# Four re-timings in an encoder trunk: a gate chunk ahead of the attention, decay tiles a score tile sooner, a seven-step age at the MLP's end, and one up chunk in token halves

## The chip, the cores and the metric

The kernel runs on one core of one Trainium2 chip. The time is the device time of that core from start to end of one execution, in microseconds (us); lower is better. The kernel before takes 1790.33 us, the median of three executions (1790.21 to 1791.44). Every duration below comes from one further execution, profiled, which took 1789.19 us with a span of 1787.3 us.

Engine names: PE multiplies matrices and transposes (a transposition is a matmul with the identity), DVE and ACT work elementwise (ACT with functions such as exp), POOL is a third elementwise engine, SP issues most of the DMA transfers. A PE matmul writes into a bank, a 128x512 buffer that ACT and DVE read; while nobody has read it, the bank can't be written again.

## The reference

Two layers over a residual stream h of 512 tokens by 1024 features. One layer computes:

```
u = RMSNorm(h)
q_a,k_a,v_a, q_r,k_r,v_r,g_r, gate_a,gate_b = split(u @ w_in)
A = dilated attention, 8 heads of 64; q,k rotated on 16 of 64 dims;
    three (window, dilation) groups merged by their softmax denominators
B = retention, 8 heads, both directions, each with its decay exp(log_gamma*(n-m));
    per-head GroupNorm, times silu(g_r)
m = sigmoid(gate_a) * (A @ w_att_out) + sigmoid(gate_b) * (B @ w_ret_out)
h = h + RMSNorm(m @ w_out)
h = h + RMSNorm(relu(RMSNorm(h) @ w_up)^2 @ w_down)        # 1024 -> 4096 -> 1024
h = h + sigmoid(RMSNorm(h) @ w_ple_gate) * RMSNorm(p[i] @ w_ple_proj)
```

All of it is float32 in and out.

## The kernel before

**Tiles and products.** The tokens lie in four tiles of 128. Each float32 operand is split into a high and a low part, and each product of a 128-deep slice takes three matmuls (high by high, high by low, low by high). Weights come as chunks of 128x1024: SP loads one (`raw`), ACT rounds it to its high part (L275), DVE or POOL forms the low part (L298). A normalised, transposed activation is `uT`: `pre_norm` (L372) normalises a token tile (`un`, L404, on DVE), and later PE transposes it in two quarters of four 128x128 blocks into the banks tp_83 and tp_84 (L412); ACT takes the high part out (L415) and DVE the low part (L416).

**Order.** PE executes its instructions in the order in which the program writes them. On the other engines a scheduler sets the order at build time from the dependences, its own estimates and priorities; at run time each engine then keeps that order. So moving something on PE can reorder DVE, ACT, POOL and SP.

**Steps.** A matmul job calls `step()` (L323) after every six matmuls. A step does two things. It takes the oldest queued transposes of a token tile if these were queued at least `age` steps ago (AGE in the input part, AGE_DN at the end of the MLP), and it lets a side generator go on by 0.94 units (`tick`). The side generator first runs the eight attention heads, then the eight retention heads; the pieces between its `yield`s stand on PE between the groups of six.

**The input part of a layer.** Value projection; four rope groups of the attention (each one two jobs of 24 matmuls, `t_job`, then rotations on DVE, L494 to L497, and a copy through DRAM by DMA). Then the side generator starts, and beside it run the main jobs: gate chunks `g_job` (24 matmuls each), four rope groups of the retention, its value projection, the output gates. One attention head (L538 on) is: four score tiles (L543, L544, two matmuls each, one step apart), for each the mask and row maximum on DVE (L547), exp with its sum on ACT (L548), reciprocal (L549) and scaling (L550) on DVE; then, a step later, four times four transposes of the scaled tiles (L562), one set of four in each step. Each set takes one block from all four scaled tiles. In every head but the first, the product with the values of the head before it (`pv`) takes the step between. One retention head: four score tiles times a decay tile (L612), the finish of the head before it (transposes at L594, L596, and the split of `retT`, L301), a product with the values, a copy of it to `yt` on ACT (L633), a step later its transposes (L638). The decay tile `T` of the next head (L581 to L587) takes POOL, DVE and at last exp on ACT (L586, 128x896).

**The MLP.** Four early up chunks (0 to 3), 28 more interleaved with seven-product matrix multiplications, then the last quarter of the down projection, `dn`, in plain form: the first half of the features for all tiles, the second half tile by tile, 24 matmuls each. After a tile's second half DVE takes the bank (L950), ACT squares (L348), DVE scales (L952) and adds to the residual (L943), ACT squares again, POOL forms 1/rms (L358), DVE normalises (L404). Its transposes follow AGE_DN steps after the tile was queued. Then comes the gate of the last block, `pg` (L319 on `uT`), tiles 0 and 1 first, in alternation, in layer 0. DN_GRP, EARLY and the ages are constants at L41 to L52. The products between (`product`, L866) also step with AGE_DN, with nothing queued at that time. EARLY is the number of first up chunks whose matmuls are done in two halves of 256 tokens (L888, 24 per half and chunk) and not in full width (24 of 512, L309).

Of the kernel before, what the change touches and what calls it, by code (L numbers as in the profile page):

```python
# [42 lines left out]
DN_GRP = ONES  # L43
PG_GRP = (PAIRS, ONES, PAIRS, ((0, 1), (2,)))
AGE = 7
AGE_DN = 6
AGE_PG = (8, 7)
AGE_VA = 7
START = (3, 5, 7)
AGE_PP = 8  # L50
EARLY = 3
EARLY_BANKS = ("s", "acc", "acc")  # L52
ROPE_POOL = ()
POOL_LOW = ("qa", "ka", "qr", "kr", "vr", "g", "ga", "ao")
# [142 lines left out]
def block(ctx: ExitStack, tc: tile.TileContext, x, pT, w, dl, gains, cs, lc, rel, eye, out):  # L197
# [306 lines left out]
    def load_qk(i, mix, h):  # L504
        g, hh = divmod(h, 4)
        q, k = stage[i, mix, g, "q"], stage[i, mix, g, "k"]
        qs = tmp.tile([P, S], F32R, name="qs", tag="qs", bufs=2)
        kk = blk("R", [P, 2, S], F32R, name="kk")
        for o in range(2):
            for hl in range(2):  # L510
                p0 = hl * 64 + o * 32
                nc.sync.dma_start(qs[p0:p0 + 32, :].bitcast(F32), q[o, hh * 32:(hh + 1) * 32, hl, :])
                nc.sync.dma_start(kk[p0:p0 + 32, :, :].bitcast(F32), k[o, hh * 32:(hh + 1) * 32, :, :])
        return qs, kk

    def att_heads(i, va, lct, attT):
        part = [None]
        qk = load_qk(i, 0, 0)

        def pv(h, pt):  # L520
            o = bank("tp")
            for k in range(NT):
                v = va[k][:, h, :, :].rearrange("p a d -> p (a d)")
                for hl in range(2):
                    nc.tensor.matmul(o, lhsT=v, rhs=pt[k][:, hl, :], start=k == 0 and hl == 0, stop=k == 3 and hl == 1)  # L525
            if h % 2 == 0:
                part[0] = t2("part")
            c = t2("cross")
            me, other = slice(64 * (h % 2), 64 * (h % 2) + 64), slice(64 - 64 * (h % 2), 128 - 64 * (h % 2))
            nc.scalar.activation(c[me], o[other], AF.Copy)  # L530
            nc.vector.tensor_tensor(part[0][me], o[me], c[me], op=ALU.add)
            if h % 2:
                b = blk("A", [P, 2, S], F32R, name="attT")
                split(b, part[0])
                attT.append(b)

        late = None
        for h in range(8):  # L538
            qs, kk = qk
            zs = []  # L540
            for t in range(NT):
                ps = bank("s")
                nc.tensor.matmul(ps, lhsT=qs[:, t * P:(t + 1) * P], rhs=kk[:, 0, :], start=True, stop=False)  # L543
                nc.tensor.matmul(ps, lhsT=qs[:, t * P:(t + 1) * P], rhs=kk[:, 1, :], start=False, stop=True)  # L544
                z = t2("z")
                nm, den, rd = col(name="nm"), col(name="den"), col(name="rd")
                nc.vector.tensor_tensor_reduce(z, ps, lct[t // 2][:, t % 2, :], -0.125, 3.0e38, ALU.add, ALU.min, nm)  # L547
                nc.scalar.activation(z, z, AF.Exp, bias=nm, scale=-1.0, accum_out=den)  # L548
                nc.vector.reciprocal(rd, den)  # L549
                nc.vector.tensor_scalar(z, z, rd, 0.5, op0=ALU.mult, op1=ALU.mult)  # L550
                zs.append(z)
                if t == 0 and h < 7:
                    qk = load_qk(i, 0, h + 1)
                yield 1
            if late:
                pv(*late)
            yield 1
            pt = []
            for k in range(NT):
                ps = bank("tp")  # L560
                for t in range(NT):
                    nc.tensor.transpose(ps[:, t * P:(t + 1) * P], zs[t][:, k * P:(k + 1) * P], ident)  # L562
                b = blk("P", [P, 2, S], F32R, name="pt")
                split(b, ps)
                pt.append(b)
                yield 1
            late = (h, pt)
        yield 1
        pv(*late)
        yield 1  # L570

    def load_v(i, h):
        v = blk("V", [P, NT, 2 * P], F32R, name="vh")
        nc.sync.dma_start(v.bitcast(F32), stage[i, "v", h // 4][:, :, h % 4, :].rearrange("t p e -> p t e"))
        return v

    def ret_heads(i, relt, gT, retT):
        late = None
        qk, vh = load_qk(i, 1, 0), load_v(i, 0)

        def decay(h):  # L581
            T = blk("X", [P, 896], name="T")
            T2 = blk("P", [P, 896], name="T2")
            nc.gpsimd.tensor_scalar(T2, relt, nlg[:, i * 16 + 8 + h:i * 16 + 9 + h], 1.0, op0=ALU.mult, op1=ALU.mult)
            nc.vector.scalar_tensor_tensor(T, relt, lg[:, i * 16 + h:i * 16 + h + 1], T2, op0=ALU.mult, op1=ALU.min)
            nc.scalar.activation(T, T, AF.Exp)  # L586
            return T  # L587

        Tn = decay(0)

        def finish(h, y3):
            ps = bank("tp")
            for t in range(NT):
                nc.tensor.transpose(ps[:, t * P:(t + 1) * P], y3[:, t, :], ident)  # L594
            z = t2("yz")
            nc.vector.tensor_tensor(z, ps, gT[h], op=ALU.mult)  # L596
            b = blk("A", [P, 2, S], F32R, name="retT")
            split(b, z, sub=nc.gpsimd if FIN_POOL else None)
            retT.append(b)

        for h in range(8):
            qs, kk = qk
            v = vh
            T = Tn
            rt = []
            for k in range(NT):
                ps = bank("s")
                nc.tensor.matmul(ps, lhsT=kk[:, 0, k * P:(k + 1) * P], rhs=qs, start=True, stop=False)  # L608
                nc.tensor.matmul(ps, lhsT=kk[:, 1, k * P:(k + 1) * P], rhs=qs, start=False, stop=True)  # L609
                z = t2("rz")  # L610
                o = 384 - P * k
                nc.vector.tensor_tensor(z, ps, T[:, o:o + S], op=ALU.mult)  # L612
                b = blk("P", [P, 2, S], F32R, name="rt")
                split(b, z, sub=nc.gpsimd if k in RT_POOL else None)
                rt.append(b)
                if k == 0 and h < 7:
                    qk, vh = load_qk(i, 1, h + 1), load_v(i, h + 1)
                yield 1
            if late:
                finish(*late)  # L620
            yield 1
            if h < 7:
                Tn = decay(h + 1)
            y = t2("y")
            y3 = y.rearrange("p (t e) -> p t e", t=NT)
            o = bank("tp")
            n = 0
            for k in range(NT):
                for a, b in HL:
                    nc.tensor.matmul(o, lhsT=v[:, k, a * P:(a + 1) * P], rhs=rt[k][:, b, :], start=n == 0, stop=n == 11)  # L630
                    n += 1
            yt = t2("yt")
            nc.scalar.activation(yt, o, AF.Copy)  # L633
            yield 1
            o = bank("tp")
            o3 = o.rearrange("p (t e) -> p t e", t=NT)
            for t in range(NT):
                nc.tensor.transpose(o3[:, t, :], yt[:, t * P:(t + 1) * P], ident)  # L638
            mv = sm.tile([P, NT, 2], F32, name="mv", tag="mv", bufs=3)
            for t in range(NT):  # L640
                st = sm.tile([P, 6], F32, name="st", tag="st", bufs=4)
                nc.vector.bn_stats(st, o3[:, t, :])
                nc.vector.bn_aggr(mv[:, t, :], st)
            ve, rs = col(NT, name="ve"), col(NT, name="rs")
            nc.vector.tensor_scalar(ve, mv[:, :, 1], 1e-5, 16.0, op0=ALU.add, op1=ALU.mult)
            nc.gpsimd.tensor_tensor(rs, ve, half, op=ALU.pow)
            for t in range(NT):
                nc.vector.tensor_scalar(y3[:, t, :], o3[:, t, :], mv[:, t, 0:1], rs[:, t:t + 1],
                                        op0=ALU.subtract, op1=ALU.mult)
            yield 1  # L650
            late = (h, y3)
        yield 1
        yield 1
        finish(*late)
        yield 1

    def one_layer(i, h):
# [70 lines left out]
        def sides():  # L728
            yield from att_heads(i, va, lct, attT)
            relt = blk("G", [P, 896], name="relt")  # L730
            nc.sync.dma_start(relt, rel)
            yield from ret_heads(i, relt, gT, retT)
# [2 lines left out]
        rope_group(i, 0, 0, ca, "k")  # L735
        rope_group(i, 0, 1, ca, "q")
        rope_group(i, 0, 1, ca, "k")
        side["gen"], side["rate"], side["owed"] = sides(), RATE, 0.0
        if i == 0:
            decays()  # L740
        cr = cs_tile(1)
        g_job(0)
        g_job(1)
        rope_group(i, 1, 0, cr, "q")
        g_job(2)
# [16 lines left out]
        h = [blk("V", [P, D], name="h") for _ in range(NT)]  # L762
# [307 lines left out]
```

## Time and profile before

| | |
|---|---|
| median of three | 1790.33 us |
| profiled execution | 1789.19 us |
| its span | 1787.3 us |
| PE busy | 1771.2 us, 99% |
| DVE, ACT, POOL busy | 1138.5, 810.8, 374.9 us |
| granted TensorE clock | full in all 40 slices |

PE is busy nearly throughout, so its idle places are few, and the waits of PE name them all. In the timeline a row is a merged run of like instructions of one engine: start, time from its start to its end, engine, line, operation, and in brackets the idle time before it with the instruction that ended it. A matmul's end is modelled and overlaps the next one's start, so the pace is read from the differences of starts.

### The profile page before, as it was taken

The page shows a single profiled execution, that of the slowest core. Times are in us where ns is not written, and L with a number is a line of the kernel's source. Part 1 is how long each engine was busy: PE and PEld are TensorE (multiplying, and loading weights), DVE is VectorE, ACT ScalarE, POOL GpSimd, SP SyncE. Part 2 cuts the span into 40 slices and gives each one's busy share as a digit, 9 for nine tenths or more (in the row PEclk, how much of TensorE's full clock was granted, in tenths as well). Part 3 has the DMA queues.
Part 4 walks back from the last instruction along what each step waited for, and adds up shares of the span by engine and source line. Part 5 has one row for each costly group of instructions (what it writes and reads, how often), then busy time and mean ns, then how long its engine had stood idle before and what let it go on. Part 6 is the DMA issues. An engine that isn't in the chain of part 4 may idle for free.

```text
span 1787.3 us, 22085 instructions
## 1 busy us (share of the span) xinstructions
PE 1771.2 (99%) x8209; PEld 1465.5 (82%) x8209; DVE 1138.5 (64%) x1760; ACT 810.8 (45%) x1280; POOL 374.9 (21%) x346
## 2 busy tenths in 40 slices
PE   9999999999999999999999999999999999999998
PEld 7878888888898888888887888888888888888887
DVE  6677768743565677674656766677444657667754
ACT  5355554422466454433443555444234664444342
POOL 3321244311141001002123212443011410000030
PEclk9999999999999999999999999999999999999999
DMA  6554564552347566551346456556332566664411
GB/s 249 182 163 157 176 206 150 164 169 95 107 142 200 153 165 162 160 184 60 129 143 216 133 164 192 181 165 191 123 106 95 165 173 156 171 173 130 165 62 69
DMA packets 87951, 274.58 MB, mean 154 GB/s; under 512 B 11937, under 2 KB 20513, under 8 KB 87842
## 3 DMA queue, kind: packets, MB, share of 16 engines
q1 hardware_dynamic: 80930, 247.99, 41.4%
q0 software_dynamic: 6912, 25.17, 8.3%
q8 instruction: 65, 1.06, 0.2%
q14 instruction: 44, 0.36, 0.1%
HBM read 239.55 MB, written 33.55 MB: 153 GB/s over the span
## 4 chain that ended last, share of the span: by engine, by line
PE 91%; DVE 3%; POOL 2%; ACT 2%; DMA 1%; issue 1%; SPq 0%; POOLq 0%; ACTq 0%
PE acc L309 29%; PE acc L319 19%; PE s L309 18%; PE acc L866 9%; PE tp L866 4%; PE tp L630 2%; PE tp L525 2%; PE tp L562 2%; PE acc L888 1%; PE tp L412 1%; PE s L543 1%; PE s L608 1%; PE s L544 1%; PE s L609 1%; PE s L888 1%
## 5 line engine op out<-in xcount | busy, mean ns | idle before, releaser
L309 PE MATMUL acc<-uT,wt 128*128 128x512 f32 x1920 | 473.5, 393 | 0.0
L309 PEld LDWEIGHTS acc<-uT,wt 128*128 128x128 f32 x1920 | 355.8, 188 | 71.4
L298 DVE TENSOR_TENSOR wt<-raw,wt 128x1024 fp32r<-128x1024 f32 (+1 forms) x222 | 285.7, 1292 | 187.3 <-ACT wt L275 186.5
L275 ACT ACTIVATE wt<-raw 128x1024 fp32r<-128x1024 f32 x279 | 293.0, 1055 | 214.3 <-PE acc L309 109.1
L309 PE MATMUL s<-uT,wt 128*128 128x512 f32 x1392 | 323.7, 389 | 0.0
L319 PE MATMUL acc<-wt,uT 128*128 128x512 f32 x1320 | 319.0, 394 | 1.3 <-DVE wt L298 0.9
L309 PEld LDWEIGHTS s<-uT,wt 128*128 128x128 f32 x1392 | 261.1, 188 | 54.1
L319 PEld LDWEIGHTS acc<-wt,uT 128*128 128x128 f32 x1320 | 245.1, 188 | 52.6 <-DVE wt L298 2.3
L298 POOL TENSOR_TENSOR wt<-raw,wt 128x512 fp32r<-128x512 f32 x118 | 160.7, 1383 | 366.3 <-ACT wt L275 316.4
L866 PE MATMUL acc<-wt,op 128*128 128x512 f32 x672 | 159.5, 389 | 0.0
L866 PEld LDWEIGHTS acc<-wt,op 128*128 128x128 f32 x672 | 126.1, 188 | 26.2
L265 POOL DMA_DIRECT2D wsum<-in_w_dram x48 | 42.5, 891 | 418.9 <-DVE wt L298 140.2
L909 ACT ACTIVATE relu<-s 128x512 f32<-128x512 f32 x60 | 35.7, 594 | 182.9 <-PE s L309 173.6
L877 DVE TENSOR_TENSOR sumP<-acc,sumP 128x512 f32<-128x512 f32 x92 | 61.7, 686 | 56.8 <-PE acc L866 56.5
L309 PE MATMUL acc<-retT,wt 128*128 128x512 f32 x384 | 89.3, 389 | 0.0
L319 PE MATMUL acc<-wt,ff 128*128 128x512 f32 x384 | 88.5, 390 | 0.0
L298 DVE TENSOR_TENSOR wt<-wsum,wt 128x1024 fp32r<-128x1024 f32 x48 | 60.5, 1261 | 40.6 <-ACT wt L275 40.6
L309 PEld LDWEIGHTS acc<-retT,wt 128*128 128x128 f32 x384 | 72.1, 188 | 15.0
L319 PEld LDWEIGHTS acc<-wt,ff 128*128 128x128 f32 x384 | 71.8, 188 | 14.8
L301 ACT ACTIVATE rt<-rz 128x512 fp32r<-128x512 f32 x64 | 40.3, 631 | 91.2 <-DVE rz L612 91.0
L866 PE MATMUL tp<-wt,op 128*128 128x512 f32 x336 | 80.7, 389 | 0.0
L866 PEld LDWEIGHTS tp<-wt,op 128*128 128x128 f32 x336 | 63.1, 188 | 13.1
(164 smaller groups left out, 2149.2 us busy)
## 6 DMA issues: line engine op xcount, KB each, us to landing
raw<-in_w_dram SPq DMA_DIRECT2D x279, 512.0 KB, 3.7
wsum<-in_w_dram POOLq DMA_DIRECT2D x48, 512.0 KB, 5.5
kk<-stk SPq DMA_DIRECT2D x128, 128.0 KB, 4.5
wsum<-in_w_dram SPq DMA_DIRECT2D x24, 512.0 KB, 3.5
stq<-rr SPq DMA_DIRECT2D x16, 512.0 KB, 4.1
qs<-stq SPq DMA_DIRECT2D x128, 64.0 KB, 2.7
stk<-rr SPq DMA_DIRECT2D x16, 512.0 KB, 3.4
stv<-vr SPq DMA_DIRECT2D x16, 512.0 KB, 3.6
```

Source lines behind the costliest of these rows:

```text
L265: nc.gpsimd.dma_start(r, rows(src[1]), accum_op=ALU.add)
L275: nc.scalar.activation(t[:, 0, :], r, AF.Copy)
L298: eng.tensor_tensor(dst, src, hi.bitcast(F32), op=ALU.subtract)
L301: nc.scalar.activation(dst[:, 0], src, AF.Copy, scale=scale)
L309: nc.tensor.matmul(ps, lhsT=t[:, a, (off + k) * P:(off + k + 1) * P], rhs=r, start=k == 0 and n == 0, stop=k == kts - 1 and n == 2)
L319: nc.tensor.matmul(ps, lhsT=lhs(a, k, t), rhs=ch[:, b, j * S:(j + 1) * S], start=first and n == 0, stop=last and n == 2)
L525: nc.tensor.matmul(o, lhsT=v, rhs=pt[k][:, hl, :], start=k == 0 and hl == 0, stop=k == 3 and hl == 1)
L562: nc.tensor.transpose(ps[:, t * P:(t + 1) * P], zs[t][:, k * P:(k + 1) * P], ident)
L630: nc.tensor.matmul(o, lhsT=v[:, k, a * P:(a + 1) * P], rhs=rt[k][:, b, :], start=n == 0, stop=n == 11)
L866: nc.tensor.matmul(ps, lhsT=op[:, a, k, j * P:(j + 1) * P], rhs=t[:, b, k * S:(k + 1) * S], start=k == 0 and n == 0, stop=k == 1 and n == 2)
L877: nc.vector.tensor_tensor(a, ps, a, op=ALU.add)
L888: nc.tensor.matmul(early[c][:, 256 * j:256 * j + 256], lhsT=t[:, a, k * P:(k + 1) * P], rhs=uT[:, b, k, 256 * j:256 * j + 256], start=k == ...
```

## The change

Five edits. The first gate chunk, `g_job(0)`, is written ahead of the side generator's start (with it the small `decays()` and the loading of the retention's cos/sin tables come one job later). The first attention head gets one more `yield` between its scores and its transposes. The next head's `decay` is written after the second score tile of a retention head, not after the finish of the head before. AGE_DN becomes 7. EARLY becomes 1, so that up chunks 1 and 2 are done in full width.

```diff
-AGE_DN = 6
+AGE_DN = 7
...
-EARLY = 3
+EARLY = 1
...
             if late:
                 pv(*late)
+            else:
+                yield 1
             yield 1
...
                 if k == 0 and h < 7:
                     qk, vh = load_qk(i, 1, h + 1), load_v(i, h + 1)
+                if k == 1 and h < 7:
+                    Tn = decay(h + 1)
                 yield 1
             if late:
                 finish(*late)
             yield 1
-            if h < 7:
-                Tn = decay(h + 1)
...
         rope_group(i, 0, 1, ca, "k")
+        g_job(0)
         side["gen"], side["rate"], side["owed"] = sides(), RATE, 0.0
         if i == 0:
             decays()
         cr = cs_tile(1)
-        g_job(0)
         g_job(1)
```

Line numbers of the changed kernel are larger by two from L557 on (by four for the few lines between the two places of `decay`); the text keeps the numbers of the kernel before, and the rows of the changed one have their own.

PE at the first attention head of layer 0, kernel before: the fourth score tile (s_82), the matmuls of `g_job(0)` and `g_job(1)` (acc_80, acc_77), and the four sets of transposes (tp_83, tp_84).

```order
L543 MATMUL s_82<-kk,qs 128x512
L544 MATMUL s_82<-kk,qs 128x512
L309 MATMUL acc_80<-uT,wt 128x512 x12
L562 MATMUL tp_83<-ident,z 128x128 x4
L309 MATMUL acc_80<-uT,wt 128x512 x6
L562 MATMUL tp_84<-ident,z 128x128 x4
```

The same place in the changed kernel:

```order
L543 MATMUL s_82<-kk,qs 128x512
L544 MATMUL s_82<-kk,qs 128x512
L309 MATMUL acc_77<-uT,wt 128x512 x18
L564 MATMUL tp_83<-ident,z 128x128 x4
L309 MATMUL acc_78<-uT,wt 128x512 x6
L564 MATMUL tp_84<-ident,z 128x128 x4
```

Eighteen matmuls of the main jobs now stand between the last score and the first transposes, where twelve stood; the spacing of the sets is the same.

ACT within the retention of layer 0, kernel before: a finish (retT), a weight rounding (wt), the exp of the decay tile (T), the copy to yt.

```order
L301 ACTIVATE retT<-yz 128x512
L275 ACTIVATE wt<-raw 128x1024
L586 ACTIVATE T<-T 128x896
L633 ACTIVATE yt<-tp_84 128x512
L701 ACTIVATE th<-acc_79 128x512
```

The changed kernel at the same head:

```order
L588 ACTIVATE T<-T 128x896
L301 ACTIVATE rt<-rz 128x512 x2
L275 ACTIVATE wt<-raw 128x1024
L703 ACTIVATE th<-acc_80 128x512
L301 ACTIVATE retT<-yz 128x512
L635 ACTIVATE yt<-tp_84 128x512
```

The exp has gone ahead of two score splits (rt), a rounding and the finish, and the copy to yt stands directly behind the finish.

DVE at the end of the MLP of layer 0, kernel before, from the residual of tile 1 on (hr): its normalisation is the first L404, that of tile 2 the second; the two pairs of L416 take tiles 0 and 1 out of the transposes' banks; acc_77 and acc_78 are the banks of tiles 2 and 3.

```order
L943 SCALAR_TENSOR_TENSOR hr<-sumP_4443,rstd,hr 128x512
L416 TENSOR_TENSOR uT<-tp_83,uT 128x4x128
L416 TENSOR_TENSOR uT<-tp_84,uT 128x4x128
L404 TENSOR_SCALAR un<-hr,rstd 128x512 x2
L950 TENSOR_TENSOR sumP_4440<-acc_77,sumP_4440 128x512
L952 TENSOR_TENSOR sumP_4440<-sumP_4440,gain 128x512
L943 SCALAR_TENSOR_TENSOR hr<-sumP_4444,rstd,hr 128x512
L943 SCALAR_TENSOR_TENSOR hr<-sumP_4440,rstd,hr 128x512
L416 TENSOR_TENSOR uT<-tp_83,uT 128x4x128
L416 TENSOR_TENSOR uT<-tp_84,uT 128x4x128
L298 TENSOR_TENSOR wt<-raw,wt 128x1024
L404 TENSOR_SCALAR un<-hr,rstd 128x512 x2
```

The changed kernel, from the same L943 on (L945 there; acc_79 is the bank of tile 2):

```order
L945 SCALAR_TENSOR_TENSOR hr<-sumP_4443,rstd,hr 128x512
L416 TENSOR_TENSOR uT<-tp_83,uT 128x4x128
L404 TENSOR_SCALAR un<-hr,rstd 128x512 x2
L416 TENSOR_TENSOR uT<-tp_84,uT 128x4x128
L952 TENSOR_TENSOR sumP_4440<-acc_79,sumP_4440 128x512
L954 TENSOR_TENSOR sumP_4440<-sumP_4440,gain 128x512
L945 SCALAR_TENSOR_TENSOR hr<-sumP_4444,rstd,hr 128x512
L945 SCALAR_TENSOR_TENSOR hr<-sumP_4440,rstd,hr 128x512
L298 TENSOR_TENSOR wt<-raw,wt 128x1024 x2
L404 TENSOR_SCALAR un<-hr,rstd 128x512 x2
L416 TENSOR_TENSOR uT<-tp_83,uT 128x4x128
L416 TENSOR_TENSOR uT<-tp_84,uT 128x4x128
```

The second L416 of tile 0 now stands behind the normalisation of tile 1, and both L416 of tile 1 stand behind two weight splits (L298) and the normalisation of tile 2.

## Rows read from the trace of the kernel before

**Rows 1.** Page, part 1: engines, busy us, share of span, instructions.
```profile
PE 1771.2 (99%) x8209; PEld 1465.5 (82%) x8209; DVE 1138.5 (64%) x1760; ACT 810.8 (45%) x1280; POOL 374.9 (21%) x346
```

**Rows 2.** Waits of PE: total us, times, longest us.
```profile
PE tp L562 <- DVE z L550: 3.2, 4, 0.9
PE tp L638 <- ACT yt L633: 2.0, 5, 0.6
PE tp L412 <- DVE uT L416: 1.7, 2, 0.9
PE tp L412 <- DVE un L404: 1.6, 4, 0.6
```

**Rows 3.** PE timeline, first attention head of layer 0, then of layer 1.
```profile
88.69 0.39 PE L543 MATMUL s<-kk,qs 128*128 128x512 f32 x1
...
91.87 0.38 PE L562 MATMUL tp<-ident,z 128*128 128x128 f32 x2
...
94.42 1.64 PE L309 MATMUL acc<-uT,wt 128*128 128x512 f32 x6
...
977.22 0.38 PE L562 MATMUL tp<-ident,z 128*128 128x128 f32 x2
...
979.50 1.64 PE L309 MATMUL acc<-uT,wt 128*128 128x512 f32 x6
```

**Rows 4.** Timeline of PE and DVE behind the second retention rope group, layer 0.
```profile
159.19 0.39 PE L543 MATMUL s<-kk,qs 128*128 128x512 f32 x1
...
161.00 0.39 PE L543 MATMUL s<-kk,qs 128*128 128x512 f32 x1
162.66 0.68 DVE L547 CUSTOM_DVE_ANT_0 z<-s,lct 128x512 f32<-128x512 f32 x1
...
163.40 0.50 PE L543 MATMUL s<-kk,qs 128*128 128x512 f32 x1 [0.42 <-DVE nm L547]
...
165.15 0.48 DVE L550 TENSOR_SCALAR z<-z,rd 128x512 f32<-128x512 f32 x1
```

**Rows 5.** Timeline of PE and ACT at a retention head, layer 0.
```profile
264.18 1.52 PE L309 MATMUL acc<-uT,wt 128*128 128x512 f32 x6
...
264.65 0.96 ACT L586 ACTIVATE T<-T 128x896 f32<-128x896 f32 x1 [0.83 <-DVE T L585]
...
265.51 0.58 ACT L633 ACTIVATE yt<-tp 128x512 f32<-128x512 f32 x1
...
266.14 0.66 PE L638 MATMUL tp<-ident,yt 128*128 128x128 f32 x4 [0.43 <-ACT yt L633]
266.55 0.71 PE L309 MATMUL acc<-uT,wt 128*128 128x512 f32 x2
```

**Rows 6.** Timeline at the first up chunks, layer 0.
```profile
514.34 3.04 PE L888 MATMUL s<-uT,wt 128*128 128x256 f32 x24
515.61 1.29 DVE L416 TENSOR_TENSOR uT<-tp,uT 128x512 fp32r<-128x512 f32 x2 [0.82 <-ACT uT L415]
...
531.62 11.07 PE L309 MATMUL s<-uT,wt 128*128 128x512 f32 x48
```

**Rows 7.** Timeline of PE and DVE at the end of the MLP, layer 0.
```profile
831.04 0.69 DVE L950 TENSOR_TENSOR sumP<-acc,sumP 128x512 f32<-128x512 f32 x1 [2.17 <-PE acc L319]
...
837.45 0.88 DVE L404 TENSOR_SCALAR un<-hr,rstd 128x512 f32<-128x512 f32 x2 [1.89 <-POOL rstd L358]
...
845.16 1.09 PE L412 MATMUL tp<-ident,un 128*128 128x128 f32 x8 [0.61 <-DVE un L404]
845.41 0.69 DVE L950 TENSOR_TENSOR sumP<-acc,sumP 128x512 f32<-128x512 f32 x1
...
850.22 4.25 PE L319 MATMUL acc<-wt,uT 128*128 128x512 f32 x18
...
852.96 0.88 DVE L404 TENSOR_SCALAR un<-hr,rstd 128x512 f32<-128x512 f32 x2 [0.45 <-POOL rstd L358]
...
861.88 1.25 PE L412 MATMUL tp<-ident,un 128*128 128x128 f32 x8 [0.90 <-DVE uT L416]
```

## The prediction, made before the changed kernel had run

> **What bounds the kernel now.** I read the page's busy shares first: PE is busy 99% of the span [rows 1], so a change counts only where PE idles or where its work gets shorter. Then the waits of PE [rows 2]: four lines hold 8.5 of the few us that it idles, and each edit but the last aims at one of them. Then the timeline at each of these places. A wait of PE is worth a little more than its idle figure, since a matmul's modelled end overlaps the next start; I therefore count by starts. The pace is .227 us for a 128x512 matmul: 88.69 to 91.87 holds two score matmuls and twelve of the main job, 3.18/14 [rows 3].
>
> The profiled execution took 1789.19 us, the median is 1790.33; I add the sum to the former and 1.14 to come to the scale of the median. A measurement of this kernel can tell about 0.2%, 3.6 us.
>
> **First attention head (gate chunk ahead, one more step).** The four transposes at 91.87 are strung out until the main job goes on at 94.42, 2.55 us, since each takes a block of a z that DVE has just scaled [rows 3]; four transposes that wait for nothing take .41 (266.14 to 266.55) [rows 5]. Lost: 2.14 in layer 0, and 979.50 - 977.22 - .41 = 1.87 in layer 1. The last transposition starts some 5.6 us behind the fourth score (88.69 to about 94.3). Now 18 and not 12 matmuls stand between, so it is due (2 + 18) x .227 + .33 = 4.87 us behind the score. If the chain kept its 5.6 us, .8 would stay in each layer. I expect it shorter: before, the scores came while DVE still worked on the rotations of the last rope group; with the gate chunk ahead they come 24 matmuls, 5.4 us, later, and the rotations are over. Term: -4.0 (bounds -4.1 and -2.5).
>
> **What the shift does behind it.** The side work now runs four steps and one tick later against the main jobs. In the order of PE two retention rope groups of a layer, not one, are followed by four score tiles with only six matmuls between, while DVE holds the rotations ahead of the mask. The row for such a burst is that of the second rope group before: scores at 159.19 and 161.00, 1.81 apart, which is eight matmuls, the next at 163.40, 2.40 apart, because both score banks wait for L547 [rows 4]. That is .59 a burst; one more in each layer makes +1.2 (0 if the rotations are through in time, 2.4 if a second score of each waits too). After another rope group comes a piece of the order in which two scores, the product with the values and the transposes stand six matmuls apart. There the tile scored last has 22 matmuls and three transposes of cover, 5.3 us; in the burst's row a tile scored at 159.19 is scaled at 165.15 + .48 = 165.63, 6.4 us later [rows 4]. That would be 1.1 late. The tile here is the second behind its rope group, the row's the first, so I take .75 in each layer, +1.5 (0 to 2.2).
>
> **Decay tiles sooner.** The Y transposes wait five times for yt, 2.0 us in all [rows 2]. At 264.18 six matmuls start, the transposes are due at 264.18 + 6 x .227 = 265.54, and start at 266.14: .60 by starts against .43 of idle. ACT was in the exp of the next decay tile from 264.65 for .96, and the copy to yt began only behind it, at 265.51 [rows 5]. Four of the five waits are of this kind, the fifth is behind a weight rounding. At 1.4 by starts for 1 of idle the five are 2.8, the four 2.4. In the changed order no exp stands right ahead of a copy to yt, so these go; but in four heads a weight rounding (L275) does, where it was two, and I give .4 back: -2.0 (bounds -2.8, all five gone, and -.8, the roundings taking over most). The exp itself is needed only by the next head's first score tile, several steps later; the POOL and DVE parts of the decay come early with it and nobody waits for them.
>
> **Seven steps at the MLP's end.** Six waits are here: four of the transposes of tiles 0 and 1 for un, 1.6 us, and two of those of tile 3 for uT, 1.7 [rows 2]. By starts that is some 4.3, 2.2 a layer. One more step, 1.36 us, is more than each of the first lasts (845.16 waited .61 [rows 7]), so the waits of tiles 0 and 1 should go. The order of DVE takes that back. The second L416 of tile 0 now stands behind the normalisation of tile 1, and both L416 of tile 1 stand behind two weight splits and the normalisation of tile 2. First effect: the transposes of tile 1 still wait, .3 for un and .55 for the bank tp_84 that the late L416 of tile 0 empties, .85 together. Second: L950 of tile 2 (845.41 before, right behind the normalisation of tile 1) comes .7 to 1.1 later, behind that L416. From L950 to the normalisation of tile 2 the chain took 852.96 - 845.41 = 7.55 us [rows 7]; so un of tile 2 is done at 846.1 + 7.55 + .88 = 854.5 or later, and the first low part of tile 1, .68 more, at 855.2. PE needs it in the pg job, which started at 850.22 [rows 7] and now would start at about 849.9 (1.1 saved, .85 lost); after six matmuls of tile 0, the third of tile 1 needs the low part, so it is due at 851.7. It waits 3.5 us. Third: the wait of tile 3's transposes (.90 at 861.88 [rows 7]) is then swallowed, as all of PE is later. New 4.35, old 2.2: +2.15 a layer, +4.3. The lower bound takes for the chain of tile 2 the 6.41 that tile 0's took (831.04 to 837.45 [rows 7]), 1.14 less: +2.0. The upper one has the tile 3 wait come back in full: +6.0. The products between carry the same constant but nothing is queued there, so they don't move.
>
> What counts in that step is that DVE doesn't pass a waiting instruction: L950 of tile 2 started at 845.41 only when the normalisation of tile 1 was through, although its bank was complete earlier [rows 7]. [...]
>
> **Up chunks in full width.** In layer 0, 514.34 to 531.62 holds 144 half-width matmuls, .120 each [rows 6]; two chunks fewer in halves are 96 x .120 = 11.52, replaced by 48 x .227 = 10.90: -.62 a layer, -1.2. What halves are for is cover: the first halves need only tiles 0 and 1. With one chunk this cover is 24 x .120 = 2.88 us in place of 8.6. The last low part is ready at 515.61 + 1.29 = 516.90, the second half starts at 514.34 + 2.88 = 517.22: .3 spare, so no stall, and if the spare went, half a us; bounds -1.3 and +.5. [...]
>
> **Sum.** -4.0 + 1.2 + 1.5 - 2.0 + 4.3 - 1.2 = -0.2; 1789.19 - 0.2 + 1.14 = 1790.1 us. All lower ends together give -6.2, 1784.1; all upper ends +7.8, 1798.1.
>
> **Rivals.**
> The MLP end gives what it says. If at run time un of tile 2 is early enough that the L416 behind it don't hold PE, the 4.3 of old waits go and nothing comes: -8.6 against the forecast, 1781.5. For it: PE alone has the waits of [rows 2]. Against it: 7.55 us from L950 to un, with two cross-engine sums of squares and POOL in it, and the pg job due 5.2 us after L950 of tile 2 at its new place. 8%.
> Small costs fall out. The bursts find DVE free (0, not 2.7), the roundings don't hurt (-2.4), the MLP end is near its lower bound (+2.4): -4.0 - 2.4 + 2.4 - 1.2 = -5.2, 1785.1. For it: before, only one of the four retention rope groups of a layer lost time to a burst. Against it: the order of DVE at the new bursts reads as in the old. 16%.
> Slower: the lateness reaches the last tile. Tile 3's bank is taken (L950) behind the same late chain on DVE; its normalisation comes 6.5 to 7.5 us later and its transposes stand at 861.88 + 2.15 = 864.0. If its L950 starts later than about 857.2 on the clock of before, un of tile 3 is later than that and PE waits a second time, some 2.3 more a layer: +9.0 in place of +4.3, 1794.8. For it: both evacuations sit in one queue. Against it: about a us of spare as I place it. 18%.
> Forecast: 58%.
>
> **Range and chances.** With the two rivals on the fast side faster by over 0.2% has .24; the slow one is .18; the forecast with its own spread (1786.7 to 1793.9) is the .58 within 0.2%. The bounds of the large unknowns, the MLP end and the bursts, make the range: 1785.5 to 1794.0, which leaves out the first rival, the edge of the slow one and the ends of the sum.
>
> **What would show it.** In the changed trace: the four transposes of the first head start within .5 us in both layers (wrong if z still ends a wait of .5 or more). Two gaps of about 2.4 between scores in each layer, not one. No wait of the Y transposes behind an exp, at most .4 in all behind roundings. In the pg job a wait of 3 us or more on uT in each layer, with L416 of tile 1 behind L404 of tile 2 on DVE; if PE shows less than 1 us there, the largest term is wrong and the time is under 1786. The up chunks' start to start shorter by .6, no wait for uT at the second half.

## The result, and the profile after

The changed kernel takes 1800.3 us (median of four, 1799.6 to 1801.17), the kernel before 1790.27: ratio 1.0056, interval 1.0039 to 1.0073. It is slower, by 10 us; the forecast was 1790.1 and its range ended at 1794.0. The profiled executions, 1801.17 and 1789.19, differ by 12.0.

To see where the time lies I add up, stage by stage, by how much each matmul's start comes later than the steady pace allows (.227 us behind a 128x512 matmul, .120 behind 256 columns, .109 behind a transposition). In us, from the two traces:

| stage, both layers | before | after | difference | forecast |
|---|---|---|---|---|
| start of the program, to 60 us | 7.5 | 8.2 | +0.6 | 0 |
| first attention heads | 4.5 | 0.2 | -4.3 | -4.0 |
| the other attention heads | 3.6 | 9.9 | +6.4 | +2.7 |
| retention, to its last head | 5.8 | 7.3 | +1.5 | -2.0 |
| end of the MLP and pg | 5.4 | 14.2 | +8.8 | +4.3 |
| up chunks (fewer half-width matmuls) | | | -1.3 | -1.2 |

The start of the program varies from 7.2 to 8.7 in the kernels run here, whatever they change, so its .6 isn't the change's. Everywhere else two kernels with the same code agree within .4 in this sum, as long as the clock is full.

The waits of PE after, total us, times, longest; the lines for z, yt, un and uT answer to [rows 2], and smaller ones are left out at the dots:

```profile
PE acc L319 <- DVE uT L416: 6.0, 3, 2.5
PE tp L564 <- DVE z L550: 3.8, 3, 1.7
PE s L543 <- DVE nm L547: 1.9, 4, 0.5
PE acc L319 <- ACT uT L415: 1.8, 2, 0.9
...
PE tp L596 <- DVE y L650: 1.2, 2, 0.6
...
PE tp L632 <- DVE rt L298: 0.8, 3, 0.3
PE tp L412 <- DVE uT L416: 0.7, 2, 0.3
```

The wait for yt is gone and that for un has shrunk out of the list, as meant. In their place stand waits of the pg matmuls for both parts of uT (ACT's high part and DVE's low part), of the last retention head for y, and of the value product for the splits rt.

**The MLP's end.** The timeline of layer 0, the same stretch as [rows 7]:

```profile
846.53 0.65 PE L412 MATMUL tp<-ident,un 128*128 128x128 f32 x4
...
847.39 0.68 DVE L952 TENSOR_TENSOR sumP<-acc,sumP 128x512 f32<-128x512 f32 x1
847.52 0.66 PE L412 MATMUL tp<-ident,un 128*128 128x128 f32 x4 [0.34 <-DVE uT L416]
...
850.77 1.52 PE L319 MATMUL acc<-wt,uT 128*128 128x512 f32 x6
...
853.22 0.73 PE L319 MATMUL acc<-wt,uT 128*128 128x512 f32 x2 [0.93 <-ACT uT L415]
...
854.91 0.88 DVE L404 TENSOR_SCALAR un<-hr,rstd 128x512 f32<-128x512 f32 x2 [0.77 <-POOL rstd L358]
855.71 1.28 DVE L416 TENSOR_TENSOR uT<-tp,uT 128x512 fp32r<-128x512 f32 x2
856.44 4.00 PE L319 MATMUL acc<-wt,uT 128*128 128x512 f32 x10 [2.48 <-DVE uT L416]
```

This is the chain that the prediction had laid out. Tile 2's bank is taken (L952) at 847.39, 7.52 us later its normalisation starts, behind it stands the L416 of tile 1, and the pg job, after six matmuls of tile 0 and two of tile 1, waits for it until 856.44. The two of tile 1 had themselves waited .93 for ACT's high part. Then comes what the prediction had not: ten matmuls take 4.00 us. The same stretch by windows, then layer 1; a row gives the stretch, its length, the busy us and in brackets the instructions of PE, PEld (the weight loads), DVE, ACT and POOL, then the granted clock, the share of the DMA engines and their GB/s:

```profile
853.00:856.00 3.00, 0.73 (x2) 0.30 (x2) 2.23 (x5) 2.55 (x4) 1.79 (x2) 1.00 0.57 184
856.00:857.00 1.00, 0.56 (x1) 0.50 (x2) 1.00 (x3) 0.00 (x0) 0.00 (x0) 0.56 1.00 250
857.00:859.60 2.60, 2.60 (x8) 2.00 (x7) 2.32 (x3) 0.72 (x2) 1.02 (x2) 0.51 0.23 95
859.60:862.00 2.40, 2.40 (x16) 2.08 (x15) 1.92 (x3) 1.13 (x4) 0.45 (x1) 1.00 0.85 299
1744.00:1747.00 3.00, 0.73 (x2) 0.30 (x2) 2.23 (x5) 2.71 (x4) 1.95 (x2) 1.00 0.58 186
1747.00:1748.00 1.00, 0.39 (x1) 0.40 (x2) 1.00 (x2) 0.00 (x0) 0.00 (x0) 0.50 0.90 254
1748.00:1751.00 3.00, 3.00 (x8) 2.32 (x8) 2.48 (x4) 0.72 (x2) 1.25 (x2) 0.50 0.29 91
1751.00:1754.00 3.00, 3.00 (x12) 2.58 (x12) 2.75 (x4) 1.59 (x4) 0.21 (x1) 0.53 0.45 162
```

Two matmuls in three us, and behind them the granted clock stands at .50 for 3.4 us in layer 0 and 6.8 us in layer 1; a 128x512 matmul then takes .427 from start to start, where it takes .227 at 1.00. By starts the waits in this stage are 4.6 in each layer (forecast: 4.35 new), and the slow stretches add 1.5 in layer 0 and 3.0 in layer 1.

### The profile page after: what moved, and what is told of

Its sections match the earlier page's. It is cut to its first block, busy times and chain, and to the rows that moved or that the text cites. A ratio compares the mean times of both kernels' runs of the same rounds, so it can differ in the third digit from the quotient of the medians.

```text
span 1799.4 us, 21916 instructions
## 1 busy us (share of the span) xinstructions
PE 1775.4 (99%) x8113; PEld 1463.6 (81%) x8113; DVE 1129.3 (63%) x1760; ACT 811.5 (45%) x1280; POOL 378.9 (21%) x346
## 4 chain that ended last, share of the span: by engine, by line
PE 89%; DVE 5%; POOL 2%; ACT 2%; issue 1%; DMA 1%; SPq 0%; ACTq 0%; DVEq 0%; POOLq 0%
PE acc L309 28%; PE acc L319 20%; PE s L309 19%; PE acc L868 8%; PE tp L868 4%; PE tp L632 2%; PE tp L564 1%; PE tp L525 1%; PE tp L412 1%; PE s L543 1%; PE s L544 1%; PE s L890 1%; PE s L610 1%; PE s L611 1%; DVE z L550 1%
## 5 line engine op out<-in xcount | busy, mean ns | idle before, releaser
L298 DVE TENSOR_TENSOR wt<-raw,wt 128x1024 fp32r<-128x1024 f32 (+1 forms) x222 | 286.3, 1295 | 180.4 <-ACT wt L275 179.2
L309 PE MATMUL s<-uT,wt 128*128 128x512 f32 x1488 | 345.4, 389 | 0.0
L319 PE MATMUL acc<-wt,uT 128*128 128x512 f32 x1320 | 323.4, 397 | 9.3 <-DVE uT L416 6.0
L309 PEld LDWEIGHTS s<-uT,wt 128*128 128x128 f32 x1488 | 279.2, 188 | 57.9
L298 POOL TENSOR_TENSOR wt<-raw,wt 128x512 fp32r<-128x512 f32 x118 | 160.2, 1378 | 354.5 <-ACT wt L275 314.9
L298 DVE TENSOR_TENSOR wt<-wsum,wt 128x1024 fp32r<-128x1024 f32 x48 | 59.7, 1244 | 45.8 <-ACT wt L275 45.8
L275 ACT ACTIVATE wt<-wsum 128x1024 fp32r<-128x1024 f32 x48 | 50.7, 1057 | 43.8 <-DMA wsum<-in_w_dram 24.9
```

The source lines that it names most:

```text
L275: nc.scalar.activation(t[:, 0, :], r, AF.Copy)
L298: eng.tensor_tensor(dst, src, hi.bitcast(F32), op=ALU.subtract)
L309: nc.tensor.matmul(ps, lhsT=t[:, a, (off + k) * P:(off + k + 1) * P], rhs=r, start=k == 0 and n == 0, stop=k == kts - 1 and n == 2)
L319: nc.tensor.matmul(ps, lhsT=lhs(a, k, t), rhs=ch[:, b, j * S:(j + 1) * S], start=first and n == 0, stop=last and n == 2)
```

## The experiments

Each is compared with the kernel before on the same chip; the ratio is that of the medians, with its 95% interval in brackets.

**AGE_DN alone.** `AGE_DN = 6` becomes 7 in the kernel before.

> Kernel before with AGE_DN 7 alone. Theory A (the wait in the pg job costs by itself, and the halved clock behind it costs again): +8.5 to +9, about 1799 us, PE waits .9 and 2.5 us in pg in each layer, and the granted clock falls to half behind the second wait in both layers. Theory B (the prediction's sum, waits alone): +4.3, 1794.6 us. If the changed kernel's loss lay mainly in the attention and retention: +2 or less.

Measured: 1799.27 us, ratio 1.0053 (1.0041 to 1.0066), +9.5. The waits in pg are 1.19 and 2.49 in layer 0, .94 and 2.48 in layer 1, and the clock falls behind them in both (mean .998 in this execution), as the first expectation has it. This edit alone makes the size of the loss.

**All edits but that one,** cut from the changed kernel.

```diff
-AGE_DN = 7
+AGE_DN = 6
```

> Changed kernel with AGE_DN back at 6. Theory A: 8.8 us under the changed kernel, about 1791.5 us, mean granted clock 1.000 instead of .997. Theory B: 4.3 under it, 1796 us.

Measured: 1791.27 us, ratio 1.0009 (1.0000 to 1.0018): 9.0 below the changed kernel. The first expectation holds. The four other edits together cost about 1.5 us.

**Filling the pause.** Into the changed kernel, ahead of tile 1's first matmuls in the pg job, come sixteen matmuls on old data, into a bank that nobody reads.

```diff
+    fill = {}
...
                 for t, ps in zip(grp, pss):
+                    if c == 0 and t == 1 and fill:
+                        dps, b = bank("s"), fill.pop("b")
+                        for _ in range(16):
+                            nc.tensor.matmul(dps, lhsT=b[:, 0, :P], rhs=b[:, 0, :], start=True, stop=True)
...
+        fill["b"] = half_f[-1]
         for hf in range(2):
```

> Changed kernel with 16 spare 128x512 matmuls (3.6 us) into an unread bank just where PE waits in the pg job, in both layers; the results are the same. If the low clock follows from the pause: clock stays full behind it, the wait shrinks to a few tenths, and the time falls by the slow stretches, 1.5 in layer 0 and 3.3 in layer 1, to about 1795.5 us, although 32 matmuls are added. If the slow stretch has another cause (the waits, the weights, the next transposes): it stays, 1800.3 us or more.

Measured: 1796.52 us, ratio 1.0039 (1.0026 to 1.0051): 3.8 us less than the changed kernel with 32 matmuls more. The windows over the fill and behind it, in layer 0 and 1:

```profile
852.00:855.00 3.00, 3.00 (x15) 2.48 (x14) 2.23 (x4) 3.00 (x6) 2.00 (x2) 1.00 0.48 162
855.00:858.00 3.00, 2.92 (x13) 2.07 (x12) 3.00 (x5) 0.78 (x3) 0.01 (x1) 1.00 0.64 193
858.00:861.00 3.00, 3.00 (x19) 2.56 (x18) 2.23 (x5) 0.64 (x2) 1.46 (x2) 1.00 0.58 202
...
1748.00:1751.00 3.00, 3.00 (x19) 2.61 (x18) 2.24 (x4) 0.96 (x3) 1.14 (x2) 1.00 0.50 180
```

The fill and the low part in layer 0 (L422 is L416 in this kernel):

```profile
851.62 3.79 PE L345 MATMUL s<-ff 128*128 128x512 f32 x16
...
855.20 1.28 DVE L422 TENSOR_TENSOR uT<-tp,uT 128x512 fp32r<-128x512 f32 x2
```

The whole stretch lies .51 earlier in this execution, and with it the low part, 855.20 against 855.71, so PE is held as long as before; but it works meanwhile, and the clock stays at 1.00. That shows that the slow stretches come from PE's pause and not from what follows it. By starts this stage's loss falls from 14.2 to 2.7, and the fill's own 32 matmuls take 7.3: 4.2 less, 1.4 of it in layer 0 and 2.9 in layer 1, where 4.8 was expected (the 3.3 in it for layer 1 is counted some .3 too high).

**Tile by tile in pg,** in the changed kernel.

```diff
-PG_GRP = (PAIRS, ONES, PAIRS, ((0, 1), (2,)))
+PG_GRP = (ONES, ONES, ONES, ((0, 1), (2,)))
```

> Changed kernel with the first pg pass of layer 0 and layer 1 tile by tile instead of tiles 0 and 1 in alternation, so that tile 1's parts are needed 24 matmuls (5.4 us) later, not 6. If the dependence on tile 1's low part is the whole cause: no wait over 1 us in pg, full clock, 1800.3 - 3.7 - 1.5 - 3.7 - 3.3 + about 2 of new waits on tile 2's transposes = 1790 us. If DVE is late with every tile: the wait moves to tile 2 or 3, 1795 or more.

Measured: 1797.09 us, ratio 1.0039 (1.0026 to 1.0051). The clock is 1.00 throughout, but the stage still loses 5.3 in each layer, in waits of at most .94: for weight splits (L298), for the bank of tile 2's transposes and of tile 3's. The second expectation holds: the lateness moved to the next tiles, and what was won against the changed kernel, 3.2, is about what the fill won, the stretches at .50.

**Seven steps with the old order on DVE.** The step's transposes get a higher build-time priority, for this age only, so that both L416 of tiles 0 and 1 stand ahead of the next tile's normalisation again. The 7.0 is seven steps; by the decimal point the code tells this age from the others.

```diff
-            soon(pending.pop(0)[1])()
+            soon(pending.pop(0)[1], PRIO + (200 if isinstance(age, float) else 0))()
-AGE_DN = 6
+AGE_DN = 7.0
```

> Kernel before with AGE_DN 7 and a higher build-time priority for the transposes' group there, so that on DVE both L416 of tiles 0 and 1 stand ahead of the next tile's normalisation, as before the change. If the order of DVE made the loss: no wait of 1 us in pg, full clock, the waits for un of tiles 0 and 1 (1.1 us a layer) gone; tile 3's wait may grow by as much, since its chain on DVE is not shortened: 1787.7 to 1790 us. If the later step itself made it: 1793 or more.

Measured: 1792.41 us, ratio 1.0014 (1.0005 to 1.0023), between the two expectations. Each against the kernel before on its own chip, +9.5 falls to +2.7: the order of DVE was 6.8 of the 9.5 us, and the step itself is no gain either: this stage loses 4.1 and 3.8 where the kernel before loses 2.9 and 2.5. Its rows in layer 0, PE and DVE:

```profile
848.10 1.09 PE L412 MATMUL tp<-ident,un 128*128 128x128 f32 x8 [0.52 <-DVE un L404]
848.35 0.68 DVE L950 TENSOR_TENSOR sumP<-acc,sumP 128x512 f32<-128x512 f32 x1
...
854.91 2.57 PE L319 MATMUL acc<-wt,uT 128*128 128x512 f32 x10 [1.14 <-DVE uT L416]
...
857.30 0.68 DVE L950 TENSOR_TENSOR sumP<-acc,sumP 128x512 f32<-128x512 f32 x1
...
864.78 0.66 PE L412 MATMUL tp<-ident,un 128*128 128x128 f32 x4 [0.95 <-DVE un L404]
```

Each tile's bank is taken behind the normalisation of the tile before, so tiles 2 and 3 follow one another on DVE 8.95 us apart (848.35 to 857.30), while PE brings one in 24 matmuls, 5.4 us. In the kernel before they are 8.35 apart (845.41 to 853.76). Later transposes don't shorten that chain, and PE waits at the next place, .95 for un of tile 3; that the chain is the reason is read from these rows and not tested.

**The head's two edits alone** (gate chunk ahead, extra step).

> Kernel before with the gate chunk ahead and the extra step alone. The first heads gain 4.0; the score bursts cost 1.2 to 1.8, the late z of the fourth score tile 3.7. If the wait for the last retention head's y (1.4 a layer) comes from the later side work: +2.8 more, 1794.0 us in all; if it comes from the decay edit: 1791.3 us.

Measured: 1793.74 us, ratio 1.0023 (1.0013 to 1.0032): the first expectation, of a shift that makes the wait at the end, holds. The last head's transposes wait for y here too.

**The gate chunk ahead alone.**

> Kernel before with the gate chunk ahead of the attention alone, without the extra step. It has the four-step shift: if that is what makes the late z and the wait for the last y, PE shows both (3.7 and 2.8 us) and the first heads still gain 1.5 or more: about 1794.5 us. If the extra step makes them: about 1788 us.

Measured: 1801.04 us, ratio 1.0066 (1.0054 to 1.0079). Both expectations miss. The first heads gain 3.2 of 4.5, but the other attention heads lose 17.1 in place of 3.6: PE waits 1.3 to 1.9 four times for z in them and 2.0 to 2.1 twice for `part` of the value product (L531), the last head 1.9 for y, and behind four of these waits the clock falls. So the four-step shift isn't a fixed price. As I read it, it decides which pieces of the side work meet the rotations on DVE, and one step more or less gives another meeting; no run tests that by itself.

**The decay tiles alone.**

> Kernel before with the decay tiles a score tile sooner alone. By the prediction's term: -2.0, 1787.8 us. If the decay's DVE part (1.15 us) queued ahead of the last scores' multiplication makes the score splits late, as read in the trace of the three-edit kernel: the five waits for yt (2.8 by starts) go and 3 to 6 us of waits of the value product on the splits come: 1790 to 1793 us.

Measured: 1793.8 us, ratio 1.0025 (1.0016 to 1.0034). That is a little above both expectations, and against the prediction's term: the stage of the retention loses 11.0 in place of 5.8. Rows at a head of layer 0:

```profile
262.10 3.52 POOL L298 TENSOR_TENSOR wt<-raw,wt 128x512 fp32r<-128x512 f32 x2 [0.27 <-ACT wt L275]
262.29 2.17 DVE L585 SCALAR_TENSOR_TENSOR T<-relt,lg,T 128x896 f32<-128x896 f32 x1
...
264.38 1.27 DVE L612 TENSOR_TENSOR rz<-s,T 128x512 f32<-128x512 f32 x2
...
266.17 1.28 DVE L298 TENSOR_TENSOR rt<-rz,rt 128x512 fp32r<-128x512 f32 x2
266.90 1.43 PE L630 MATMUL tp<-rt,vh 128*128 128x512 f32 x5 [0.39 <-DVE rt L298]
```

DVE's part of the next decay tile now stands ahead of the multiplication of this head's last two scores (L612), and the value product waits for their splits. It also takes longer there: in eight of the sixteen heads 2.16 to 2.28 us, with POOL at work beside it (here on a weight split), and 1.14 to 1.15 in the others; in the kernel before one of sixteen was so long, in the changed kernel three.

**One up chunk in halves alone.**

> Kernel before with one up chunk in token halves, not three. By the paces of the rows (.120 for a half, .227 for a full one): -.6 a layer, -1.2, about 1788.5 us, and no wait at the second half. [...] If tile 3's low part is late: a wait there and no gain.

Measured: 1788.94 us, ratio .9991 (.9982 to 1.0000): -1.0, with no wait at the second half. The rows' paces were right.

**Three edits: extra step, early decay, halves.**

> Kernel before with three of the five edits: the extra step of the first head (main jobs not moved), the early decay tiles, one up chunk in halves. Theory A (what cost was the four-step shift and AGE_DN 7, not these): first heads -2.7 (.8 and .5 us of wait stay), decay -1.2 to -2.4, halves -1.2, no wait for the last head's y: about 1784.5 us. Rival (every shift of the side work disturbs the scores and the tail alike): within a us of 1790.

Measured: 1793.72 us, ratio 1.0021 (1.0012 to 1.0030), which neither expectation has. I had taken the early decay for a gain; it cost as above (the retention loses 14.7 in place of 5.8, 4.1 of it at the last heads' y). The attention without the four-step shift did get better: the heads behind the first lose 2.4 in place of 3.6.

**The extra step with the phase kept.** With one up chunk in halves, the first head gets its extra step and gives one back behind its last transposes:

```diff
+            else:
+                yield 1
             yield 1
...
                 pt.append(b)
-                yield 1
+                if h or k < 3:
+                    yield 1
```

> Kernel before with one up chunk in halves and the extra step in the first head, taken back by one step less behind that head's transposes, so that all later side work stands where it stood. First heads -2.1 - 1.9 + .8 + .5 = -2.7, halves -1.0 (as measured alone), nothing else: 1786.2 us. If the later places move all the same (order of DVE): within a us of 1789.

Measured: 1785.32 us, ratio .9973 (.9962 to .9984). It beats both kernels: 4.4 us less than the kernel before, where some 3.7 was expected. The first head of layer 0:

```profile
89.90 4.25 PE L309 MATMUL acc<-uT,wt 128*128 128x512 f32 x18
93.98 0.49 PE L564 MATMUL tp<-ident,z 128*128 128x128 f32 x3
95.11 0.33 PE L564 MATMUL tp<-ident,z 128*128 128x128 f32 x1 [0.64 <-DVE z L550]
```

Three transposes go at once, the last waits .64; the first heads lose 1.75 in place of 4.45, and every stage behind them loses what it lost before.

**All that looked good.** The last kernel with the seven steps in the old order, and tile 3's bank taken ahead of tile 2's normalisation.

> One up chunk in halves, extra step with the phase kept, and AGE_DN 7 with the old order on DVE, and tile 3's bank taken ahead of tile 2's normalisation. The first two -3.7; the MLP end 0 to -2.5 with tile 3's bank taken some .9 us sooner: 1783.5 to 1786.2 us. If tile 3's wait takes all: 1786.2 or more.

Measured: 1787.7 us, ratio .9986 (.9977 to .9995): 2.4 worse than without the seven steps, about as in their own run (2.7). Tile 3's bank is now taken 7.87 us behind tile 2's in layer 0, not 8.95, but its normalisation starts 7.73 us behind that and not 6.93, and most of the gain is gone. Best stays the kernel above.

## Why the prediction was wrong

**The MLP's end, +8.8 and not +4.3.** This is the step that failed most. Its mechanism was right in its main links: the order of DVE, the late bank of tile 2, a wait in pg of 3.7 a layer by starts where 3.5 was worked out (1.1 of it on ACT's high part, which I hadn't named). The sum priced a pause of PE by its length alone, and left what follows it at nothing without a reason. By waits alone the term would have come to about +3.8. The runs show that the pause is paid a second time, by the stretch at a clock of .50 behind it, 1.5 and 3.0 us; the fill took just that away. My third rival had the size, +9.0 for this term, from a second wait of tile 3; that wait didn't come (its transposes start at 866.63, un is there at 864.65), so the size was met by accident.

**The other attention heads, +6.4 and not +2.7.** Of the two terms the bursts were right: two in each layer, .6 to .7 each by starts. The late z was mis-sized. I took .75 a layer from a row in which the tile stood first behind its rope group; in the changed kernel:

```profile
131.94 0.39 PE L543 MATMUL s<-kk,qs 128*128 128x512 f32 x1
132.03 2.57 POOL L298 TENSOR_TENSOR wt<-raw,wt 128x512 fp32r<-128x512 f32 x2 [5.18 <-ACT wt L275]
132.11 0.68 DVE L494 TENSOR_TENSOR ra<-acc,cst 128x512 f32<-128x512 f32 x1
...
133.41 1.48 DVE L550 TENSOR_SCALAR z<-z,rd 128x512 f32<-128x512 f32 x1
...
136.60 0.67 DVE L547 CUSTOM_DVE_ANT_0 z<-s,lct 128x512 f32<-128x512 f32 x1
...
138.60 0.49 DVE L550 TENSOR_SCALAR z<-z,rd 128x512 f32<-128x512 f32 x1
...
139.14 0.33 PE L564 MATMUL tp<-ident,z 128*128 128x128 f32 x1 [1.72 <-DVE z L550]
```

The fourth score starts at 131.94, and five rotation instructions (L494, L495, L497 and again L494, L495) stand ahead of its L547: 7.15 us from score to z against 5.3 of cover, 1.9 a layer, and .5 more at another place of layer 1. Where 0 to 2.2 was allowed for both layers, the trace has 4.3. It was a place where the order of DVE could be read, and I scaled a neighbour's row instead of counting the instructions. Counting alone would not have given all of it: the third tile's scaling between them, at 133.41, takes 1.48 us where the fourth's takes .49, beside the weight split on POOL, and the same happens in layer 1. So about one of the 1.9 us is this longer instruction, an estimate from these rows.

**The retention, +1.5 and not -2.0.** The waits for yt went entirely, 2.8 by starts. The sentence that failed is that the DVE part of the decay comes early "and nobody waits for them": in the run of the decay tiles alone the scores' multiplication behind it does, and the value product with it. In the changed kernel the value product waits three times for the splits, 1.5 us by starts, and a score tile once, .5; the run of the head's edits alone has none of these waits. And the side work, four steps later, reaches the end of the main jobs: the last head's transposes come eighteen matmuls behind the statistics' input, as before, but DVE now puts a gate (L721) and a weight split ahead of the last steps of the statistics:

```profile
370.34 0.65 DVE L721 SCALAR_TENSOR_TENSOR fT<-tha,acc 128x512 f32<-128x512 f32 x1
...
371.00 1.19 DVE L298 TENSOR_TENSOR wt<-raw,wt 128x1024 fp32r<-128x1024 f32 x1
372.11 0.17 DVE L647 TENSOR_SCALAR ve<-mv 128x4 f32<-128x4 f32 x1
...
373.87 1.29 PE L596 MATMUL tp<-ident,y 128*128 128x128 f32 x4 [0.62 <-DVE y L650]
```

That is 1.4 a layer, 2.8, for which the prediction had no term. The run of the head's edits alone shows it without the early decay, and the decay tiles alone don't show it, so it belongs to the shift.

**What held.** The first heads (-4.3, forecast -4.0): all four transposes start at the steady spacing. The halves (-1.0 by time, -1.3 by count, forecast -1.2). The first rival, a full gain at the MLP's end, was rightly held unlikely. The range failed because three terms missed on the same side; even all upper ends together, 1798.1, lie below the result. Each is a stretch in which DVE, not PE, sets the pace, and each had its upper end worked out from a wait and not from a queue.

## What to carry to other kernels

Here PE is 99% busy, and moving work between its queue places was paid on DVE, which didn't pass a waiting instruction: in layer 0 of the changed kernel it idled .77 us ahead of tile 2's normalisation at 854.91, though ACT was through with the high part for the L416 behind it at 853.66, and PE waited 2.48 us for that L416. So count the instructions that a new order puts ahead of the one waited for, and don't scale a neighbour's row. A pause of PE may cost more than its length: here a clock of .50 followed eight of ten pauses of 1.9 to 2.5 us, and in the changed kernel it cost another 1.5 us in layer 0 and 3.0 in layer 1, so put that into the upper end, and keep PE busy over a pause that can't be removed. Win cover locally and give the step back at once, so that the rest of the schedule keeps its phase: that and the halves made 4.4 us here, while the head's two edits with a moved phase lost 4.0. The extra step alone, not given back, wasn't run.

## What the hardware showed that I had not expected

The granted clock falls to .50 behind pauses of PE, but not each time. In the traces of all runs PE has ten single pauses of 1.9 to 2.5 us: two in the changed kernel, two in the run of AGE_DN alone, six in that of the gate chunk alone. A clock of .50 follows eight, and in the run of the gate chunk alone a wait of 1.94 for z is followed by it in layer 1 (clock .51 from 1011 to 1014) and not in layer 0. Ten pauses of 1.7 us, the late z of the changed kernel and of four runs with it, are followed by none. The low stretch lasts about 3.4 us in each place but one, where it is 6.8. Shorter pauses in a row stand ahead of two more falls. The first head of layer 0 loses the same 2.1 us to strung-out transposes in the kernel before, in the run with seven steps in the old order and in that with the decay alone; behind it the clock stays at 1.00 in the first and stands at .50 for about 3.4 us in the other two:

```profile
95.00:98.00 3.00, 3.00 (x18) 2.48 (x17) 1.91 (x3) 2.15 (x4) 0.00 (x0) 1.00 0.74 175
```

```profile
96.00:99.00 3.00, 3.00 (x11) 2.41 (x10) 1.69 (x3) 1.75 (x3) 0.00 (x0) 0.50 0.78 168
```

The first is the kernel before, the second the old-order run: 18 matmuls and transposes in three us against 11. So part of the scatter between executions of one kernel may be this clock, and the record of each execution's mean granted clock bears it out. Beside the last four runs, 16 executions of the kernel before at 1.000 have a median of 1789.45 us, and 13 at .999 have 1790.57; the gate chunk alone goes from 1799.86 at .999 to 1805.56 at .995. In some others (the decay tiles alone, for one) it doesn't separate them, and no run held the clock. The kernel with the phase kept, whose pauses at the heads are shorter, shows 1.000 in all seven executions (1784.88 to 1785.83); against the 1789.45 it gains 4.1, so some of the 4.4 is this.

DVE's part of a decay tile took 2.17 us beside a weight split on POOL (the rows of the decay run) and 1.14 in the three-edit kernel, where POOL did nothing at that time:

```profile
259.92 1.14 DVE L587 SCALAR_TENSOR_TENSOR T<-relt,lg,T 128x896 f32<-128x896 f32 x1
```

The other traces say the same. In all fourteen together, 668 scalings of z (L550) with POOL idle beside them take .47 to .49 us each, and 141 with POOL at work over more than half of their time .49 to 1.54, half of them 1.09 or more; of these the traces before and after have 96, at .47 to .49, and 20, at .49 to 1.51. Rotations that read a bank of PE (L494, L495) keep their .67 to .69 beside POOL. No run here took POOL's work away to separate it from other causes.
